# Sample states of an mLSTM step fetched two halves ahead, with GpSimd's stores and the memory input queued behind the last fetch

## The chip, the cores and the metric

The kernel runs on one core of one Trainium2 chip. The metric is device time in microseconds (us) of one execution; the time before is the median of three runs. Names of the engines in the profile: PE is TensorE (matmul; PEld its weight loads), DVE is VectorE, ACT is ScalarE, POOL is GpSimd, SP is SyncE, which here only issues DMAs.

## The reference

One layer of a hybrid decoder, in f32, on 256 prompt tokens and 8 sample tokens (one new token for each of 8 sequences), model width 2048. What matters here is the mLSTM of the sample tokens, four heads with keys of 128 and values of 256:

```python
def layer(x, conv_buf, h0, C0, n0, m0, mk, mv, ...):
    z = rmsnorm(x, g_mix) @ w_in                 # inputs of both head groups
    ... # causal conv, RG-LRU: y_rg
    q, k, v, logi, logf = ...                    # slices of z
    h_ml, C_new, n_new, m_new = mlstm(q, k, v, logi, logf, C0, n0, m0)
    y_ml = rmsnorm(h_ml, g_ml_out) * sigmoid(z[o])
    x = x + concat([y_rg, y_ml]) @ w_out
    x = x + cross_attention(rmsnorm(x, g_xa), mk, mv) @ w_xa_o
    x = x + (silu(xf @ w_ffn_gate) * (xf @ w_ffn_up)) @ w_ffn_down
# mlstm for one token, per sequence and head (sc, D from the gates):
#   C_new = sc * C + D * k v^T ;  n_new = sc * n + D * k
#   h = (q C_new) / max(|q n_new|, exp(-m))
```

The outputs are the prompt's and samples' activations and all new states, among them `o_sc` (C_new of the samples, 4 MB), `o_sn` (n_new), `o_h`, `o_cp`, `o_cs` (RG-LRU and conv states). The prompt's memory keys and values are made in the layer from `memT`; the samples' come from caches (`kcT`, `vcT`).

## The kernel before

The work is a list of steps on TensorE, one for each block of 128 output columns of a weight matrix (`w_in`, `w_out`, `w_q`, ...). A step reads 1 MB of weights, which SyncE loads as two halves of 512 KB (`raw`, five buffers). Each half is cast on ScalarE (`w<-raw`, the high part) and split on VectorE (`w<-raw,w`, the low part) into one of four `w` buffers; a product of f32 numbers is then three matmuls of high and low parts (`mm3`), 48 in a step. The splits of a step are made while the step before it runs.

All else is side work: generators (`rg_gen` for the RG-LRU, `ml_gates`, `ml_prompt`, `ml_values`, `ml_heads` and `ml_sample` for the mLSTM, `mem_gen` for the memory input, and others), from which `pump` takes pieces between steps by estimated times. A scheduler then orders the instructions of VectorE, ScalarE, GpSimd and TensorE by its own estimate; SyncE's stay as written. Each engine runs its instructions in the order so found, and a waiting one holds up all behind it. `tc.issue_after(x)` puts an instruction behind x. Tiles named `B` come from one pool of 26 buffers, so a DMA into a `B` waits until the buffer's last user is done.

`ml_prompt` makes, for each head, decay weights `E` (two `tensor_scalar`, one Exp, a mask product), the weighted scores `Pm` and the weighted keys `kw` (kept in `kb`); `ml_heads` multiplies `Pm` with the transposed values `vts`. Keys and values are kept in DRAM (`kept_k`, `kept_v`) for the prompt's state, which is made at the end of the kernel.

`ml_sample` works through the samples' states in eight halves, one for each head h and each group b4 of four sequences. It first writes the scaled keys `kd` and the queries of all heads and sequences as 64 rows to DRAM (`scr`). For a half, `fetch` then loads 512 KB of state (`C`, from `c0T`) and the half's key and query rows, each broadcast to all 128 partitions (`kq`, from `scr`). For each sequence ScalarE makes `dw` (two copies of the key row, scaled by a value), VectorE updates the state (`B<-B,bcs,dw`) and sums query times state twice (`ds<-B,B`); the new half goes out with `o_sc`. Before the change half n+1 is fetched when half n begins. All DMAs of this generator, and those of `memT`, `kcT`, `vcT`, are issued by GpSimd, whose queue is in order too.

Of the kernel before, what the change touches and what calls it, by code (L numbers as in the profile page):

```python
# [13 lines left out]
AF = mybir.ActivationFunctionType  # L14
# [3 lines left out]
P = 128  # L18
D = 2048
KC = D // P  # L20
T = 256
NS = 8
N = T + NS
RGB = 8
H = 4
# [17 lines left out]
STEP = object()  # L43
# [52 lines left out]
def layer_kernel(ctx: ExitStack, tc, xT, memT, vec, wrg, w_in, w_out, w_q, w_k, w_v, w_o,  # L96
# [3 lines left out]
    act, dve, pe = Engine(nc.scalar, price_act), Engine(nc.vector, price_dve), Engine(nc.tensor, price_pe)  # L100
    pool_e, sp = nc.gpsimd, nc.sync
# [17 lines left out]
    def B(shape, dt=F32):  # L119
        return sb.tile(shape, dt, tag="B", bufs=NB, name=nm("B"))  # L120
# [5 lines left out]
    def ltmp(w=N):  # L126
        return tmp(w, "lt")
# [381 lines left out]
    cpo = const.tile([P, RGB, 3], F32, name="cpo")  # L509
    cso = const.tile([P, RGB, NS, 3], F32, name="cso")  # L510
# [34 lines left out]
    def rg_gen():  # L545
# [41 lines left out]
        for q in range(2):  # L587
# [3 lines left out]
            act.activation(hlast[:, 4 * q: 4 * q + 4, :], h.tile(q)[:, :, T - 1: N], AF.Copy)  # L591
        pool_e.dma_start(o_h, hlast)
        pool_e.dma_start(o_cp, cpo)
        pool_e.dma_start(o_cs, cso)
        yield 0.3
# [190 lines left out]
    def ml_prompt():  # L786
# [13 lines left out]
        for h in range(H):  # L800
# [12 lines left out]
            dve.tensor_scalar(E[:, 256:384], bc[:, P:T], gcol[:, 1, h: h + 1], 0.0, op0=OP.add, op1=OP.min)  # L813
            act.activation(E, E, AF.Exp)
            if h == 0:
# [52 lines left out]
    def ml_sample():  # L868
# [3 lines left out]
        ks, qs = qk.tile(1)[:, :, T:N], qk.tile(0)[:, :, T:N]  # L872
        sc, Dg = bcs[:, :, 0:8], bcs[:, :, 8:16]
        x = ltmp(64)
        kd, qc = (x[:, o: o + 32].rearrange("p (h b) -> p h b", b=NS) for o in (0, 32))
        dve.tensor_mul(kd, ks, Dg)
        dve.tensor_copy(qc, qs)
        n0 = V("n0", 0, 32).rearrange("p (h b) -> p h b", b=NS)
        dve.tensor_mul(snew, n0, sc)
        dve.tensor_add(snew, snew, kd)  # L880
        pool_e.dma_start(o_sn, snew)

        dve.tensor_mul(ssum[:, 1], snew, qc)
        yield 0.6
# [9 lines left out]
        def fetch(h, b4):  # L894
            C, kq = B([P, 4, 2, P]), B([P, 2, 4, P])
            pool_e.dma_start(C, c0T[h, :, b4 * 4: b4 * 4 + 4])
            for j in range(2):
                r0 = j * 32 + h * 8 + b4 * 4
                src = scr[r0: r0 + 4, :].rearrange("b d -> (b d)")
                pool_e.dma_start(kq[:, j].rearrange("p b d -> p (b d)"), src.partition_broadcast(P))  # L900
            return C, kq

        ahead = fetch(0, 0)
        yield STEP
        for h in range(H):
            while ml.get("vn", 0) < 2 * h + 2 or "last" not in ml:
                yield STEP
            for b4 in range(2):
                C, kq = ahead
                n = 2 * h + b4 + 1  # L910
                if n < 2 * H:
                    ahead = fetch(n // 2, n % 2)
                for bb in range(4):
                    b = b4 * 4 + bb
                    t2 = sb.tile([P, 264], F32, tag="dw", bufs=2, name=nm("dw"))[:, 0: T]
                    t2 = t2.rearrange("p (v d) -> p v d", d=P)
                    for vb in range(2):
                        act.activation(t2[:, vb, :], kq[:, 0, bb, :], AF.Copy,
                                       scale=ml["v"](2 * h + vb)[:, T + b: T + b + 1])
                    with tc.issue_after(ml["last"].ins):  # L920
# [6 lines left out]
                    yield 0.8  # L927
                pool_e.dma_start(o_sc[h, :, b4 * 4: b4 * 4 + 4], C)
        yield 0.1
# [165 lines left out]
    def mem_gen():  # L1095
        raw = Arr(KC, T)
        for i in range(4):
            pool_e.dma_start(raw.tile(i), memT[:, i * 4: i * 4 + 4, :])
        yield STEP
# [375 lines left out]
    for i, (src, cols, pef, evf, need) in enumerate(steps):  # L1475
# [49 lines left out]
        if i == 57:  # L1525
            PACE["full"] = False
        if i == 44:
            pool_e.dma_start(kept_k, ml["kb"])
            for q in range(2):
                pool_e.dma_start(kept_v[q], ml["vts"][q])  # L1530
        if i == 40:
# [119 lines left out]
```

## Time and profile before

| | |
|---|---|
| median of three runs | 1449.22 us (1447.74 to 1449.48) |
| profiled execution | 1447.88 us, span of its trace 1445.9 us |
| TensorE busy | 1429.2 us (99%), clock granted 0.998 |
| VectorE, ScalarE, GpSimd busy | 1050.8 (73%), 796.9 (55%), 127.9 us (9%) |
| DMA | 329.17 MB, mean 228 GB/s |

Times inside the trace count from the start of the span. A row of the timeline gives the start, the time taken, engine, line, operation, out<-in by tile names, shape, how many alike follow each other, and in brackets how long the engine had idled before and what ended that. Most rows have line 61, that of a helper which records every operation, so tiles tell more than lines.

### The profile page before, as it was taken

How to read it: one execution, taken by the hardware profiler on the slowest of the kernel's cores; microseconds unless marked ns; L12 is line 12 of the kernel's file. 1: busy time of each engine (PE TensorE's matmuls, PEld its weight loads, DVE VectorE, ACT ScalarE, POOL GpSimd, SP SyncE). 2: the span in 40 equal slices, each digit the busy share in tenths (PEclk: the TensorE clock that was granted, in tenths of full speed). 3: DMA queues.
4: the chain of work that ended last, by engine and by line, in shares of the span. 5: the costliest groups of instructions: out<-in, count | busy, mean ns of one | idle time of the engine just before them, and what ended most of it. 6: DMA issues, size and time to landing. Idle time of an engine off the chain costs nothing.

```text
span 1445.9 us, 29975 instructions
## 1 busy us (share of the span) xinstructions
PE 1429.2 (99%) x11979; PEld 1405.4 (97%) x11979; DVE 1050.8 (73%) x2014; ACT 796.9 (55%) x1289; POOL 127.9 (9%) x203
## 2 busy tenths in 40 slices
PE   9999999999999999999999999999999999999997
PEld 9999899999999999899999999999999999999997
DVE  7967798998899999977676656555665655556565
ACT  7678786765556666655544444434444434444474
POOL 0001220000225433300000000000000000000000
PEclk9999999999999999999999999999999999999999
DMA  9745897557789887856555555555555555555573
GB/s 291 235 172 188 297 361 277 176 177 274 280 334 383 318 303 263 338 173 216 193 194 197 194 198 195 194 200 192 196 198 190 201 193 192 201 191 197 169 239 128
DMA packets 100764, 329.17 MB, mean 228 GB/s; under 512 B 11056, under 2 KB 19936, under 8 KB 100624
## 3 DMA queue, kind: packets, MB, share of 16 engines
q1 hardware_dynamic: 84480, 272.09, 54.2%
q0 software_dynamic: 15424, 54.22, 10.1%
q8 instruction: 93, 1.52, 0.4%
q10 hardware_dynamic: 720, 0.95, 0.2%
q14 instruction: 47, 0.39, 0.1%
HBM read 314.36 MB, written 12.86 MB: 226 GB/s over the span
## 4 chain that ended last, share of the span: by engine, by line
PE 56%; DVE 1%; issue 1%; DMA 0%; ACT 0%; POOL 0%; DVEq 0%; POOLq 0%; ACTq 0%
PE mm L61 56%; PE ax L61 1%; DVE B L61 1%; DVE dw L61 0%; DMA o_v<-B 0%; POOL ds L1200 0%; DVE w L61 0%; DVE t L61 0%; ACT B L61 0%; ACT dw L61 0%; ACT t L61 0%; DVE ax L61 0%; ACT ds L61 0%; DVE rstd L61 0%; DVEq L1628 0%
## 5 line engine op out<-in xcount | busy, mean ns | idle before, releaser
L61 PE MATMUL mm<-B,w 128*128 128x264 f32 (+1 forms) x10960 | 1281.9, 279 | 1.8 <-DVE w L61 1.7
L61 PEld LDWEIGHTS mm<-B,w 128*128 128x128 f32 x10960 | 1261.3, 189 | 9.9 <-DVE w L61 2.3
L61 DVE TENSOR_TENSOR w<-raw,w 128x1024 fp32r<-128x1024 f32 (+1 forms) x522 | 625.2, 1200 | 299.0 <-ACT w L61 298.3
L61 ACT ACTIVATE w<-raw 128x1024 fp32r<-128x1024 f32 (+1 forms) x522 | 534.8, 1028 | 514.6 <-PE mm L61 353.3
L61 PE MATMUL mm<-w,B 128*128 128x512 f32 x384 | 86.9, 380 | 0.1
L61 PEld LDWEIGHTS mm<-w,B 128*128 128x128 f32 x384 | 70.7, 190 | 9.6 <-DVE w L61 0.5
L1542 POOL TENSOR_TENSOR B<-B,rstd 128x264 f32<-128x264 f32 x4 | 2.8, 735 | 802.0 <-ACT B L61 802.0
L61 DVE TENSOR_TENSOR t<-mm,rstd 128x264 f32<-128x264 f32 x96 | 41.6, 434 | 28.4 <-PE mm L61 28.3
L61 DVE SCALAR_TENSOR_TENSOR B<-B,dw 128x256 f32<-128x256 f32 x128 | 54.3, 478 | 3.2 <-ACT dw L61 3.0
L61 DVE TENSOR_TENSOR xres<-xres,mm 128x264 f32<-128x264 f32 (+1 forms) x81 | 34.2, 424 | 24.6 <-PE mm L61 24.6
L61 DVE SCALAR_TENSOR_TENSOR dw<-B,qsm,dw 128x256 f32<-128x256 f32 x96 | 48.7, 513 | 2.4 <-ACT dw L61 1.6
L61 PE MATMUL ax<-B,B 128*128 128x256 f32 (+3 forms) x276 | 44.6, 302 | 1.9 <-DVE B L61 1.0
L1200 POOL TENSOR_TENSOR ds<-dw,ds 128x256 fp32r<-128x256 f32 x32 | 35.6, 1114 | 107.1 <-ACT ds L61 107.0
L61 PEld LDWEIGHTS ax<-B,B 128*128 128x128 f32 x276 | 38.0, 191 | 4.7 <-DVE B L61 1.6
L61 ACT ACTIVATE B<-xres,vecs 128x264 fp32r<-128x264 f32 (+1 forms) x64 | 32.2, 503 | 4.5 <-DVE xres L61 2.7
L61 ACT ACTIVATE dw<-B,qsm 128x256 f32<-128x256 f32 x32 | 16.3, 508 | 24.6 <-issue 10.5
L1189 POOL DMA_DIRECT2D B<-kcT x32 | 17.3, 542 | 139.1 <-DVE B L61 126.2
L61 ACT ACTIVATE t<-xres 128x264 f32<-128x264 f32 (+1 forms) x53 | 21.0, 408 | 14.0 <-DVE xres L61 13.9
L61 ACT ACTIVATE dw<-B,B 128x128 f32<-128x128 f32 x64 | 21.2, 393 | 11.8 <-DMA B<-scr 8.5
L61 DVE SCALAR_TENSOR_TENSOR B<-xres,vecs,B 128x264 fp32r<-128x264 f32 x48 | 23.4, 489 | 4.1 <-ACT B L61 4.1
L61 ACT ACTIVATE dw<-ax,dw 128x256 f32<-128x256 f32 x32 | 15.0, 469 | 18.8 <-DVE dw L61 17.8
L61 ACT ACTIVATE B<-t 128x264 fp32r<-128x264 f32 (+1 forms) x60 | 24.1, 409 | 1.8 <-DVE t L61 1.8
(182 smaller groups left out, 684.9 us busy)
## 6 DMA issues: line engine op xcount, KB each, us to landing
raw<-w_gu SPq DMA_DIRECT2D x176, 512.0 KB, 4.1
raw<-w_d SPq DMA_DIRECT2D x80, 512.0 KB, 3.9
raw<-w_in SPq DMA_DIRECT2D x74, 512.0 KB, 5.2
raw<-w_out SPq DMA_DIRECT2D x32, 512.0 KB, 4.0
raw<-w_q SPq DMA_DIRECT2D x32, 512.0 KB, 5.9
B<-kcT POOLq DMA_DIRECT2D x32, 512.0 KB, 8.7
B<-vcT POOLq DMA_DIRECT2D x32, 512.0 KB, 10.0
raw<-w_k SPq DMA_DIRECT2D x32, 512.0 KB, 5.1
```

Source lines behind the costliest of these rows:

```text
L61: return f(*a, **k)
L1189: pool_e.dma_start(kc, kcT[h, b])
L1200: pool_e.tensor_sub(ws[:, 1], acc, ws[:, 0].bitcast(F32))
L1542: e.tensor_mul(st["y"](c), st["y"](c), r)
```

## The change

The states of the first two halves are loaded at the start of `ml_sample`, as soon as the gates are there. The key and query rows are laid out so that one broadcast DMA brings both for a half. Two fetches run ahead; the next one is issued behind a half's work, and the half's store `o_sc` behind that fetch. The first use of the rows on ScalarE (`dw`) stands behind the first Exp of `ml_prompt`. The stores of kept keys and values, of `o_h`, `o_cp`, `o_cs` and `o_sn` move behind the last `o_sc`, and the loads of memory input behind the last kept store.

```diff
@@ rg_gen
-        pool_e.dma_start(o_h, hlast)
-        pool_e.dma_start(o_cp, cpo)
-        pool_e.dma_start(o_cs, cso)
@@ ml_prompt
-            act.activation(E, E, AF.Exp)
+            ml.setdefault("exp", act.activation(E, E, AF.Exp))
@@ ml_sample
+        def load(h, b4):
+            C = B([P, 4, 2, P])
+            pool_e.dma_start(C, c0T[h, :, b4 * 4: b4 * 4 + 4])
+            return C
+
+        loaded = [load(0, 0), load(0, 1)]
         x = ltmp(64)
-        kd, qc = (x[:, o: o + 32].rearrange("p (h b) -> p h b", b=NS) for o in (0, 32))
+        kd = ltmp(32).rearrange("p (h b) -> p h b", b=NS)
...
         dve.tensor_mul(kd, ks, Dg)
-        dve.tensor_copy(qc, qs)
+        dve.tensor_copy(x4[:, :, :, 0], by4(kd))
+        dve.tensor_copy(x4[:, :, :, 1], by4(qs))
...
-        pool_e.dma_start(o_sn, snew)
...
         def fetch(h, b4):
-            C, kq = B([P, 4, 2, P]), B([P, 2, 4, P])
-            pool_e.dma_start(C, c0T[h, :, b4 * 4: b4 * 4 + 4])
-            for j in range(2):
-                r0 = j * 32 + h * 8 + b4 * 4
-                src = scr[r0: r0 + 4, :].rearrange("b d -> (b d)")
-                pool_e.dma_start(kq[:, j].rearrange("p b d -> p (b d)"), src.partition_broadcast(P))
+            C = loaded.pop(0) if loaded else load(h, b4)
+            kq = B([P, 2, 4, P])
+            r0 = (2 * h + b4) * NS
+            src = scr[r0: r0 + NS, :].rearrange("b d -> (b d)")
+            ml["fetch"] = pool_e.dma_start(kq.rearrange("p j b d -> p (j b d)"), src.partition_broadcast(P))
             return C, kq
 
-        ahead = fetch(0, 0)
+        ahead = [fetch(0, 0), fetch(0, 1)]
...
-                C, kq = ahead
-                n = 2 * h + b4 + 1
-                if n < 2 * H:
-                    ahead = fetch(n // 2, n % 2)
+                C, kq = ahead.pop(0)
+                n = 2 * h + b4 + 2
                 for bb in range(4):
...
-                    for vb in range(2):
-                        act.activation(t2[:, vb, :], kq[:, 0, bb, :], AF.Copy,
-                                       scale=ml["v"](2 * h + vb)[:, T + b: T + b + 1])
+                    with tc.issue_after(ml["exp"].ins):
+                        for vb in range(2):
+                            act.activation(t2[:, vb, :], kq[:, 0, bb, :], AF.Copy,
+                                           scale=ml["v"](2 * h + vb)[:, T + b: T + b + 1])
...
-                pool_e.dma_start(o_sc[h, :, b4 * 4: b4 * 4 + 4], C)
+                if n < 2 * H:
+                    ahead.append(fetch(n // 2, n % 2))
+                with tc.issue_after(ml["fetch"].ins):
+                    last = pool_e.dma_start(o_sc[h, :, b4 * 4: b4 * 4 + 4], C)
+        while min(ml.get("pn", 0), ml.get("vtn", 0)) < H:
+            yield STEP
+        with tc.issue_after(last.ins):
+            pool_e.dma_start(kept_k, ml["kb"])
+            for q in range(2):
+                ml["kept"] = pool_e.dma_start(kept_v[q], ml["vts"][q])
+            pool_e.dma_start(o_h, hlast)
+            pool_e.dma_start(o_cp, cpo)
+            pool_e.dma_start(o_cs, cso)
+            pool_e.dma_start(o_sn, snew)
@@ mem_gen
-            pool_e.dma_start(raw.tile(i), memT[:, i * 4: i * 4 + 4, :])
+            with tc.issue_after(ml["kept"].ins):
+                pool_e.dma_start(raw.tile(i), memT[:, i * 4: i * 4 + 4, :])
@@ layer_kernel, the loop over the steps
-        if i == 44:
-            pool_e.dma_start(kept_k, ml["kb"])
-            for q in range(2):
-                pool_e.dma_start(kept_v[q], ml["vts"][q])
```

What this does to the order on the engines. GpSimd's queue before, from the rows' store to the third half's fetch (`c0T` loads a state, the loads from `scr` bring its rows, one DMA for keys and one for queries):

```order
L892 DMA scr_1803<-lt_197_1801 64x128
L896 DMA B_208_1881<-c0T 128x1024
L900 DMA B_209_1882<-scr_1803 128x512 x2
L592 DMA o_h<-hlast_94 128x72
L896 DMA B_219_1977<-c0T 128x1024
L900 DMA B_220_1978<-scr_1803 128x512 x2
L1530 DMA kept_v_106<-B_177_1625 128x1032
L928 DMA o_sc<-B_208_1881 128x1024
L1528 DMA kept_k_105<-B_187_1708 128x1024
L928 DMA o_sc<-B_219_1977 128x1024
L896 DMA B_266_2272<-c0T 128x1024
L900 DMA B_267_2273<-scr_1803 128x512 x2
```

The same place after, and on to the store of the third half (`B_267`) with the sixth half's row (`B_328`) behind it:

```order
L874 DMA B_179_1629<-c0T 128x1024
L874 DMA B_180_1631<-c0T 128x1024
L897 DMA scr_1808<-lt_200_1806 64x128
L904 DMA B_211_1886<-scr_1808 128x1024
L904 DMA B_212_1888<-scr_1808 128x1024
L874 DMA B_267_2267<-c0T 128x1024
L904 DMA B_268_2269<-scr_1808 128x1024
L934 DMA o_sc<-B_179_1629 128x1024
...
L874 DMA B_327_2641<-c0T 128x1024
L934 DMA o_sc<-B_267_2267 128x1024
L904 DMA B_328_2643<-scr_1808 128x1024
```

The third half's fetch now stands ahead of the first state store and of both kept stores; a later row, the sixth half's, stands behind the third half's store. On ScalarE before, around the first Exp of `ml_prompt` (the row `B_207<-B_207`), with the first half's `dw` copies ahead of two weight casts:

```order
L61 ACTIVATE B_177_1625<-ax_196_1795 128x2x256
L61 ACTIVATE dw_221_1982<-B_209_1882,B_180_1636 128x128 x2
L61 ACTIVATE dw_237_2077<-B_209_1882,B_180_1636 128x128 x2
L61 ACTIVATE w_210_1887<-raw_193_1773 128x8x128
L61 ACTIVATE hlast_94<-B_204_1872 128x36
L61 ACTIVATE w_211_1890<-raw_194_1775 128x8x128
L61 ACT_TABLE_LOAD
L61 ACTIVATE B_207_1880<-B_207_1880 128x384
L61 ACTIVATE B_187_1708<-B_186_1707,B_207_1880 128x128 x2
```

And after:

```order
L61 ACTIVATE B_177_1625<-ax_199_1800 128x2x256
L61 ACTIVATE w_213_1891<-raw_196_1778 128x8x128
L61 ACTIVATE hlast_94<-B_207_1877 128x36
L61 ACTIVATE w_214_1894<-raw_197_1780 128x8x128
L61 ACT_TABLE_LOAD
L61 ACTIVATE B_210_1885<-B_210_1885 128x384
L61 ACTIVATE dw_222_1978<-B_211_1886,B_183_1641 128x128 x2
L61 ACTIVATE dw_238_2073<-B_211_1886,B_183_1641 128x128 x2
L61 ACTIVATE B_190_1713<-B_189_1712,B_210_1885 128x128 x2
```

The four `dw` copies moved from ahead of the two weight casts to behind the Exp. On VectorE the order changes only from the fourth half on; where the seventh half is updated (`B_350` before, `B_351` after), before the change, from one weight split to the next:

```order
L61 TENSOR_TENSOR w_345_2755<-raw_324_2644,w_345_2755 128x8x128
L61 SCALAR_TENSOR_TENSOR ds_364_2904,nums_108<-B_326_2649,B_327_2650 128x128
L61 SCALAR_TENSOR_TENSOR B_350_2815<-B_350_2815,bcs_96,dw_378_2993 128x256
L61 SCALAR_TENSOR_TENSOR ds_366_2911,nums_108<-B_326_2649,B_327_2650 128x128
L61 TENSOR_TENSOR acc_rg_95<-acc_rg_95,t_333_2672 128x264
L61 TENSOR_TENSOR t_343_2748<-mm_336_2681,rstd_91 128x264
L61 SCALAR_TENSOR_TENSOR B_350_2815<-B_350_2815,bcs_96,dw_387_3066 128x256
L61 SCALAR_TENSOR_TENSOR ds_364_2904,nums_108<-B_326_2649,B_327_2650 128x128
L61 TENSOR_TENSOR w_346_2758<-raw_325_2646,w_346_2758 128x8x128
```

After, the last twelve rows ahead of the split that corresponds to the one after those:

```order
L61 SCALAR_TENSOR_TENSOR ds_365_2895,nums_108<-B_327_2641,B_328_2643 128x128
L61 SCALAR_TENSOR_TENSOR ds_367_2902,nums_108<-B_327_2641,B_328_2643 128x128
L61 TENSOR_TENSOR B_207_1877<-B_207_1877,t_344_2740 128x264
L61 SCALAR_TENSOR_TENSOR ds_378_2980,nums_108<-B_351_2806,B_352_2808 128x128
L61 SCALAR_TENSOR_TENSOR B_351_2806<-B_351_2806,bcs_96,dw_388_3056 128x256
L61 SCALAR_TENSOR_TENSOR ds_380_2987,nums_108<-B_351_2806,B_352_2808 128x128
L61 SCALAR_TENSOR_TENSOR B_351_2806<-B_351_2806,bcs_96,dw_390_3063 128x256
L61 SCALAR_TENSOR_TENSOR ds_378_2980,nums_108<-B_351_2806,B_352_2808 128x128
L61 TENSOR_TENSOR acc_rg_95<-acc_rg_95,t_345_2744 128x264
L61 SCALAR_TENSOR_TENSOR ds_380_2987,nums_108<-B_351_2806,B_352_2808 128x128
L61 SCALAR_TENSOR_TENSOR ds_389_3060,nums_108<-B_351_2806,B_352_2808 128x128
L61 TENSOR_TENSOR w_347_2750<-raw_326_2639,w_347_2750 128x8x128
```

Eleven of the seventeen operations that stand between two splits there are shown; before, seven stand between the two.

More of the change, by code (lines that the diff above doesn't have):

```diff
@@ L873, in ml_sample @@
         sc, Dg = bcs[:, :, 0:8], bcs[:, :, 8:16]
+        def load(h, b4):
[3 more added lines that the diff above has]
+        loaded = [load(0, 0), load(0, 1)]
         x = ltmp(64)
-        kd, qc = (x[:, o: o + 32].rearrange("p (h b) -> p h b", b=NS) for o in (0, 32))
+        kd = ltmp(32).rearrange("p (h b) -> p h b", b=NS)
+        by4 = lambda t: t.rearrange("p h (g b) -> p h g b", b=4)
+        x4 = x.rearrange("p (h g j b) -> p h g j b", g=2, j=2, b=4)
         dve.tensor_mul(kd, ks, Dg)
-        dve.tensor_copy(qc, qs)
+        dve.tensor_copy(x4[:, :, :, 0], by4(kd))
+        dve.tensor_copy(x4[:, :, :, 1], by4(qs))
         n0 = V("n0", 0, 32).rearrange("p (h b) -> p h b", b=NS)
@@ L880, in ml_sample @@
         dve.tensor_add(snew, snew, kd)
-        pool_e.dma_start(o_sn, snew)
-        dve.tensor_mul(ssum[:, 1], snew, qc)
+        dve.tensor_mul(ssum[:, 1], snew, qs)
         yield 0.6
```

## The prediction

> **What bounds the kernel now.** I read the page's busy times first, then the busy time by stage, then what TensorE waits for, then the rows of the engines that it waits for.
>
> ```profile
> PE 1429.2 (99%) x11979; PEld 1405.4 (97%) x11979; DVE 1050.8 (73%) x2014; ACT 796.9 (55%) x1289; POOL 127.9 (9%) x203
> ```
>
> TensorE is busy for 1429.2 of 1445.9 us, so a change elsewhere can only win what is in its gaps. By stage (columns: stretch, length, PE, PEld, DVE, ACT, POOL busy, clock, DMA share, GB/s):
>
> ```profile
> 100.00:140.00 40.00, 39.55 (x335) 38.80 (x335) 25.28 (x47) 33.15 (x62) 4.87 (x9) 1.00 0.49 165
> 140.00:180.00 40.00, 38.05 (x302) 36.25 (x301) 30.00 (x86) 28.60 (x72) 8.51 (x16) 1.00 0.87 295
> 180.00:220.00 40.00, 38.24 (x331) 37.44 (x330) 40.00 (x143) 32.70 (x78) 9.10 (x17) 1.00 0.97 366
> 220.00:260.00 40.00, 40.00 (x359) 40.00 (x358) 33.07 (x76) 23.66 (x36) 0.00 (x0) 1.00 0.69 248
> ```
>
> The sample states are worked through in the second and third rows. TensorE idles 0.45 + 1.95 + 1.76 = 4.16 us in 100 to 220, and not at all after it. The list of its waits from 100 to 240 us has 4.1 us, and its own rows show where they lie:
>
> ```profile
> PE mm L61 <- DVE w L61: 1.7, 2, 1.5
> PE ax L61 <- DVE B L61: 1.5, 3, 0.7
> PE ax L61 <- ACT B L61: 0.9, 1, 0.9
> ```
> ```profile
> 139.74 0.66 PE L61 MATMUL ax<-ident,B 128*128 128x128 f32 x4 [0.45 <-DVE B L61]
> 148.02 1.14 PE L61 MATMUL ax<-B,B 128*128 128x258 f32 x4 [0.39 <-DVE B L61]
> 158.86 1.14 PE L61 MATMUL ax<-B,B 128*128 128x258 f32 x4 [0.65 <-DVE B L61]
> ...
> 170.61 5.65 PE L61 MATMUL mm<-B,w 128*128 128x264 f32 x48
> 177.11 1.57 PE L61 MATMUL ax<-B,B 128*128 128x258 f32 x6 [0.86 <-ACT B L61]
> ...
> 195.50 11.68 PE L61 MATMUL mm<-B,w 128*128 128x264 f32 x96 [0.15 <-DVE w L61]
> 208.71 16.24 PE L61 MATMUL mm<-B,w 128*128 128x264 f32 x142 [1.53 <-DVE w L61]
> ```
>
> Six gaps, 0.45 + 0.39 + 0.65 + 0.86 + 0.15 + 1.53 = 4.03 us: the most that this change can remove. Behind them stand two waits of ScalarE for a broadcast row (`B<-scr`, the `kq` tile):
>
> ```profile
> 135.21 1.28 ACT L61 ACTIVATE dw<-B,B 128x128 f32<-128x128 f32 x4 [3.56 <-DMA B<-scr]
> 136.39 1.04 ACT L61 ACTIVATE w<-raw 128x1024 fp32r<-128x1024 f32 x1
> ...
> 173.77 1.28 ACT L61 ACTIVATE dw<-B,B 128x128 f32<-128x128 f32 x4 [4.96 <-DMA B<-scr]
> 174.96 1.04 ACT L61 ACTIVATE w<-raw 128x1024 fp32r<-128x1024 f32 x1
> ...
> 176.49 0.57 ACT L61 ACTIVATE B<-ax 128x512 f32<-128x512 f32 x1
> ```
>
> Behind each wait stands the cast of a weight half, which VectorE then splits; after the second also the copy (176.49) that TensorE waits for at 177.11. VectorE takes the delay over:
>
> ```profile
> 137.47 1.23 DVE L61 TENSOR_TENSOR w<-raw,w 128x1024 fp32r<-128x1024 f32 x1 [1.55 <-ACT w L61]
> ...
> 174.50 1.07 DVE L61 SCALAR_TENSOR_TENSOR B<-B,bcs,dw 128x256 f32<-128x256 f32 x2 [4.43 <-ACT dw L61]
> ...
> 207.41 1.25 DVE L61 TENSOR_TENSOR w<-raw,w 128x1024 fp32r<-128x1024 f32 x1
> 208.55 0.51 DVE L61 SCALAR_TENSOR_TENSOR B<-B,bcs,dw 128x256 f32<-128x256 f32 x1
> 208.94 0.31 DVE L61 SCALAR_TENSOR_TENSOR ds<-B,B 128x128 f32<-128x128 f32 x1
> 209.15 0.11 DVE L61 DVE_READ_ACCUMULATOR ds<-B,B 128x1 f32 x1
> ```
>
> After 4.43 idle us at 174.5 it is busy without a break through 180 to 220 (40.00 above), and the split that starts at 207.41 is the one that TensorE waits for at 208.71.
>
> **Why the second row was late.** GpSimd's queue, where the DMA issues wait in order:
>
> ```profile
> 156.30 0.54 POOL L928 DMA_DIRECT2D o_sc<-B  x1 [8.58 <-DVE B L61]
> 161.42 0.53 POOL L1528 DMA_DIRECT2D kept_k<-B  x1 [4.58 <-ACT B L61]
> 163.66 0.53 POOL L928 DMA_DIRECT2D o_sc<-B  x1 [1.71 <-DVE ds L61]
> 164.19 0.53 POOL L896 DMA_DIRECT2D B<-c0T  x1
> 164.71 1.08 POOL L900 DMA_DIRECT2D B<-scr  x2
> ```
>
> The third half's two fetches stand behind two state stores and a `kept_k` store, each waiting for its data; they issue at 164.19 and 164.71, only 4 us before ScalarE wants the row (173.77 − 4.96 = 168.81).
>
> **The change part by part.** *First use behind the Exp.* The four `dw` copies of the first half move behind ScalarE's first Exp. The 3.56 us wait goes, and the cast at 136.39 can run as soon as its `w` buffer and weights are there. VectorE then starts the split of 137.47 up to 1.55 us earlier. From that split on VectorE and ScalarE hand work to each other, so the lead should last to the gaps at 139.74, 148.02 and 158.86. These need 0.45, 0.84 and 1.49 us of lead in turn, since TensorE itself comes earlier by what the gaps before gave. Late next: the `dw` copies, 1.28 us of ScalarE, now stand between the Exp and the two key copies. They delay the key copies only, which nothing waits for before the store at the end. The bounds: none of the 1.49 (another wait takes over) or all of it. I take 0.45 + 0.39 + half of 0.65 = 1.16, as a lead of 1.55 against a need of 1.49 leaves nothing for a slip.
>
> *The third fetch no longer behind `kept_k` and the stores.* In the new order the third half's two fetches stand ahead of the first state store. What they wait for then is a free buffer: by the program's buffers, the end of the last head's score matmuls, here the group at 154.83.
>
> ```profile
> 154.83 0.82 PE L61 MATMUL ax<-B,B 128*128 128x256 f32 x4
> ...
> DMA to landing us min/median/max: 3.9/10.6/14.6
> ```
>
> So they issue at about 156. The second line is the time to landing of the row fetches (and of the rows' own store) before. In the new order nothing else is queued ahead of them by then, so the low end is nearest, with 512 KB in one DMA in place of two of 256 KB; even the median gives 167, before 168.81. The 4.96 us wait goes, and with it the 0.86 us gap. VectorE starts the third half 4.43 us earlier. How much of that is left where TensorE waited? The new order on VectorE puts four updates, nine sums and four other operations between two weight splits, where it had fewer. By the spacing of the rows above (1.14 split, 0.39 update, 0.21 sum) and 0.35 taken for the others, between the two, this is 1.14 + 1.56 + 1.89 + 1.40 = 6.0 us, and adding up all operations since 174.50 in the two orders the split after it stands 2.4 us later than before, the next one 0.4 us later. TensorE uses up a split in 5.65 / 2 = 2.83 us. The split of 207.41 was 1.53 us late; with 4.43 − 0.4 = 4.0 us of lead, less 1.0 us by which TensorE comes earlier (0.86 + 0.15), it is 1.5 us early. The one before it gets 4.43 − 2.4 − 1.0 = 1.0 us more than it had, and it was in time. So I take all of 0.86 + 0.15 + 1.53 = 2.54; the bounds are 0 and 2.54.
>
> *States fetched earlier, one broadcast in place of two.* Two state fetches go out ahead of the rows' store and no longer behind it; the DMA share in 100 to 140 was 0.49, so the weight loads hide them, at nothing. Were that cover gone, a load would come a few us later, with the casts ahead of TensorE by a whole step. Eight issues of 0.54 us go from GpSimd, which was 9% busy. One small copy more on VectorE (below 0.3 us) falls in a stage where it is 25.28 of 40 us busy: nothing.
>
> *Stores moved behind the last state store.* `kept_k`, both `kept_v`, `o_h`, `o_cp`, `o_cs`, `o_sn`, then memory input: about 1.7 MB of stores come ahead of the four memory loads. What was there:
>
> ```profile
> 218.92 0.53 POOL L1098 DMA_DIRECT2D B<-memT  x1 [5.74 <-ACT t L61]
> 267.63 0.40 ACT L61 ACTIVATE lt<-B 128x256 f32<-128x256 f32 x1
> 220.00:230.00 10.00, 10.00 (x92) 10.00 (x91) 6.82 (x15) 6.57 (x8) 0.00 (x0) 1.00 1.00 390
> 230.00:240.00 10.00, 10.00 (x92) 10.00 (x91) 9.86 (x25) 7.45 (x15) 0.00 (x0) 1.00 0.58 193
> ```
>
> The memory input is first read at 267.63, nearly 50 us after the last issue. At 390 − 193 = 197 GB/s beside the weights the extra 1.7 MB take some 9 us, so the memory input comes by about 236. Its cover is those 30 us; nothing else waits for these stores. The weight loads share the transfers in this stretch without a gap on TensorE at 390 GB/s, so I price them at nothing.
>
> The sum: 1.16 + 2.54 = 3.7 us. Against the profiled execution (1447.88 us, span 1445.9) that is 1444.2; this execution lies 1.34 us below the median of the three runs, 1449.22, so the median to expect is 1445.5 us, 0.26% less.
>
> **The rivals.** *Only the later gaps go* (chance 0.22). If the head's chain of Exp, scores and PSUM banks sets the three early gaps, the lead of 1.55 us is lost and 2.54 us remain: 1446.7. For it speaks that the last two of them come 12 and 23 us after ScalarE's wait; against it that all three end on VectorE, which is 30.00 of 40 us busy there.
>
> *VectorE takes it back* (0.11): after 340 us it is the fuller engine.
>
> ```profile
> 400.00:460.00 60.00, 60.00 (x469) 58.06 (x468) 58.09 (x149) 36.10 (x61) 22.21 (x33) 1.00 0.95 354
> 460.00:520.00 60.00, 60.00 (x331) 54.15 (x330) 58.49 (x147) 37.87 (x75) 23.62 (x28) 1.00 0.82 304
> 520.00:600.00 80.00, 79.58 (x481) 72.62 (x480) 76.68 (x197) 51.23 (x102) 29.21 (x45) 1.00 0.88 333
> ```
>
> If it were bound there by something that doesn't start earlier, all 3.7 us would turn into a wait of TensorE near 590 to 620: 1449.2. Against it: that work starts with the queries, which TensorE paces, and 220 to 260 leaves VectorE 7 us to fall into step.
>
> *A fetch behind a store* (0.10). The sixth half's row now stands behind the third half's store, and the eighth's behind the fourth's. With the third half started at 174.50 − 4.43 = 170.1, its updates end near 176, where the sixth row is issued; adding up the operations in the new order, ScalarE needs it near 187, eleven microseconds later. If it lands later, ScalarE waits with weight casts behind it, as at 173.77, and all of the wait beyond the 1.0 to 1.5 us of lead comes back as gaps. At the longest landing, 14.6, that is 3.6 − 1.2 = 2.4 us of the 3.7 gained: 1447.9. From about 19 us on it decides: 8 us of wait are 6.7 us of gaps, 3.0 more than the gain, 1452.2. For it speaks the DMA share of 0.97 in 180 to 220; against it that fetches of two halves leave this stretch.
>
> *More is hidden than the gaps show* (0.02). The PEld column falls short by 1.20 + 3.75 + 2.56 = 7.5 us in 100 to 220, against 4.16 in the PE column; if all of it were lost time that the change gives back, the time would be 1441.7. Against it: 48 matmuls take 5.65 us in the disturbed stretch at 170.61, and the products in plain f32 that stand between them run long on one weight load, so I trust the gaps. [...] No run here shows yet which of the two the time follows.
>
> *It doesn't do what it says* (0.05): the buffer for the third half is not free before 164, and the fetch stays where it was. Then only the early 1.16 remain: 1448.1.
>
> **How the numbers follow.** The forecast, both terms, has 0.50; its own range is 1444.3 (all 4.03 us, and a little of the runs' spread) to 1446.6. A difference under 0.2%, 2.9 us, is about what a measurement of this kernel can't tell from none. The forecast lies on the fast side of that bound in five of six cases, the first rival in three of ten: faster 0.42 + 0.07, and 0.02 for the hidden time, roughly 0.50. Slower: the third rival with a landing past 19 us, 0.06. Same: the rest, 0.44. The range 1443.9 to 1449.3 takes in the first two rivals, the third at the longest landing seen and the fourth; it leaves out the slower end and the 7.5 us of the weight loads.
>
> **What would show it.** Right: no wait of ScalarE for `B<-scr`; VectorE's idle time before the third half gone; the third fetch issued before 157; no gap of TensorE over 0.3 us from 130 to 215; the same stage rows after 400. Wrong: a wait for `B<-scr` near 185 or 200, a gap near 590 to 620, a wait for `raw` in 210 to 240, or the early three gaps still there.

## The result: 0.5% faster, twice what was forecast

The changed kernel takes 1441.53 us (median of five runs, 1441.14 to 1442.52), the kernel before 1449.16 in the same series: ratio 0.995, 95% interval 0.9939 to 0.9961. That is 7.6 us less, where 3.7 were forecast (1445.5, range 1443.9 to 1449.3). The profiled execution after took 1442.52 us (span 1439.5), the one before 1447.88 (span 1445.9).

The busy times of the profile after, then the stages 100 to 220 us by the same columns as before, then all waits of TensorE:

```profile
PE 1426.8 (99%) x11979; PEld 1404.9 (98%) x11979; DVE 1050.3 (73%) x2015; ACT 796.5 (55%) x1289; POOL 124.1 (9%) x195
```
```profile
100.00:140.00 40.00, 40.00 (x342) 39.43 (x341) 26.83 (x51) 33.10 (x61) 1.67 (x3) 1.00 0.49 167
140.00:180.00 40.00, 39.35 (x320) 38.19 (x320) 34.34 (x105) 34.18 (x93) 7.38 (x14) 1.00 0.82 282
180.00:220.00 40.00, 40.00 (x356) 39.81 (x354) 37.38 (x124) 29.70 (x61) 9.03 (x17) 1.00 0.97 368
```
```profile
PE ax L61 <- ACT w L61: 1.4, 2, 1.1
PE mm L61 <- DVE pad L61: 1.1, 1, 1.1
PE ax L61 <- DVE B L61: 0.7, 1, 0.7
PE ax L61 <- ACT t L61: 0.3, 1, 0.3
```

Of the six gaps between 130 and 220 one is left, the 0.65 us of the head products, now at 157.49. VectorE is no longer full from 180 to 220 (37.38 of 40). The third half's fetch issues behind the last score matmuls, ahead of the first state store, and ScalarE starts the half without a wait:

```profile
154.57 0.53 POOL L874 DMA_DIRECT2D B<-c0T  x1 [21.51 <-PE ax L61]
155.09 0.53 POOL L904 DMA_DIRECT2D B<-scr  x1
155.61 0.54 POOL L934 DMA_DIRECT2D o_sc<-B  x1
```
```profile
167.35 1.26 ACT L61 ACTIVATE dw<-B,B 128x128 f32<-128x128 f32 x4
...
187.18 1.26 ACT L61 ACTIVATE dw<-B,B 128x128 f32<-128x128 f32 x4
...
198.52 1.26 ACT L61 ACTIVATE dw<-B,B 128x128 f32<-128x128 f32 x4
```

To see where the time went I matched each weight split of VectorE with the same split in the other trace and took the difference of their starts. The changed kernel is 0.25 us later at 111 us, 5.23 earlier at 277, and 6.68 earlier from 650 to the end. So 5.48 us come from the stage 111 to 277 and 1.45 from 277 to 650, where nothing was expected. The rest up to 7.6 lies in the spread of executions: the start of the kernel, up to 111 us, differs by up to 1.7 us between traces whose order there is nearly the same.

The gain in the late stage has a cause that stands in the rows of before. GpSimd there, before:

```profile
571.77 0.56 POOL L1189 DMA_DIRECT2D B<-kcT  x1
574.47 0.53 POOL L1193 DMA_DIRECT2D B<-vcT  x1 [2.13 <-issue]
574.99 0.53 POOL L1189 DMA_DIRECT2D B<-kcT  x1
```

and after (that trace is 5.6 us earlier there):

```profile
566.16 0.55 POOL L1206 DMA_DIRECT2D B<-kcT  x1
566.70 0.54 POOL L1210 DMA_DIRECT2D B<-vcT  x1
567.23 0.53 POOL L1206 DMA_DIRECT2D B<-kcT  x1
...
581.38 0.57 POOL L1268 DMA_DIRECT2D o_k<-t  x1
584.43 0.54 POOL L1206 DMA_DIRECT2D B<-kcT  x1 [2.49 <-issue]
```

Some 2 us in which GpSimd waits for nothing that the profile shows stand ahead of the 54th load of `kcT` or `vcT` before, and ahead of the 61st after. Counted along its queue both are the 115th DMA issue; the change has eight issues fewer ahead of it. (Another unexplained stretch, 4.05 us at 404.04 before and 4.04 at 398.81 after, stays with its load.) Behind the 2 us before the change, key loads landed late (the 57th load at 588.89 us, against 585.46 in the changed kernel; table below), and TensorE waited for the samples' scores:

```profile
585.22 0.38 PE L61 MATMUL ax<-ds,onesr 128*128 128x256 f32 x1 [0.24 <-ACT ds L61]
...
588.63 0.38 PE L61 MATMUL ax<-ds,onesr 128*128 128x256 f32 x1 [0.17 <-POOL ds L1200]
```
```profile
619.29 0.38 PE L61 MATMUL ax<-ds,onesr 128*128 128x256 f32 x1 [0.24 <-POOL ds L1200]
```

None of these three waits is left after the change.

### The profile page after: what moved, and what is told of

It is laid out like the page before. It is cut to its first block, busy times and chain, and to the rows that moved or that the text cites. A ratio compares the mean times of both kernels' runs of the same rounds, so it can differ in the third digit from the quotient of the medians.

```text
span 1439.5 us, 29961 instructions
## 1 busy us (share of the span) xinstructions
PE 1426.8 (99%) x11979; PEld 1404.9 (98%) x11979; DVE 1050.3 (73%) x2015; ACT 796.5 (55%) x1289; POOL 124.1 (9%) x195
## 3 DMA queue, kind: packets, MB, share of 16 engines
q8 instruction: 93, 1.52, 0.4%
## 4 chain that ended last, share of the span: by engine, by line
PE 69%; DVE 1%; issue 0%; ACT 0%; POOL 0%; DVEq 0%; POOLq 0%; ACTq 0%
PE mm L61 67%; PE ax L61 2%; DVE B L61 0%; DVE w L61 0%; DVE dw L61 0%; POOL ds L1217 0%; DVE t L61 0%; ACT w L61 0%; ACT t L61 0%; DVE ax L61 0%; ACT dw L61 0%; ACT ds L61 0%; DVE rstd L61 0%; DVE osm L61 0%; DVEq L1641 0%
## 5 line engine op out<-in xcount | busy, mean ns | idle before, releaser
L61 ACT ACTIVATE ds<-dw 128x256 fp32r<-128x256 f32 x32 | 13.3, 415 | 21.8 <-DVE dw L61 21.8
```

Of the source, the lines that this page charges most:

```text
L61: return f(*a, **k)
```

## The experiments

Shifts are against the trace of before, in us (minus is earlier), over the two stages; the last two columns are what TensorE's two columns lack of 130 us from 110 to 240. "115th issue" tells which of the loads of `kcT` and `vcT` is the 115th DMA on GpSimd's queue. All traces are single ones: a wait of 0.4 us near 436 that comes and goes between kernels of the same order (below) moves the second stage by that much.

| kernel | median (before beside it) | ratio, 95% | 111 to 277 | 277 to 650 | 115th issue | PE idle | PEld idle |
|---|---|---|---|---|---|---|---|
| before | | | 0 | 0 | 54th | 4.15 | 7.25 |
| changed | 1441.53 (1449.16) | 0.9939 to 0.9961 | -5.48 | -1.45 | 61st | 0.65 | 2.31 |
| first use only | 1446.46 (1448.94) | 0.9975 to 0.9992 | -2.09 | +0.73 | 54th | 2.54 | 5.21 |
| two ahead only | 1451.08 (1448.94) | 1.0008 to 1.0026 | +1.18 | +0.40 | 54th | 5.14 | 8.53 |
| stores only | 1446.94 (1448.85) | 0.9977 to 0.9994 | -0.41 | -0.87 | 54th | 3.66 | 6.86 |
| one row only | 1448.98 (1448.94) | 0.9990 to 1.0008 | +1.52 | -1.43 | 61st | 5.39 | 8.78 |
| changed, no first use | 1444.03 (1448.94) | 0.9954 to 0.9979 | -3.42 | -1.41 | 61st | 1.96 | 4.30 |
| changed, stores back | 1448.70 (1448.85) | 0.9993 to 1.0010 | +3.19 | -1.81 | 61st | 5.31 | 7.79 |
| changed, two rows | 1442.21 (1448.07) | 0.9945 to 0.9972 | -5.83 | -1.31 | 54th | 0.65 | 2.11 |
| changed, 8 DMAs more | 1443.70 (1448.85) | 0.9952 to 0.9977 | -5.49 | -0.74 | 54th | 0.65 | 2.31 |
| changed, 14 memsets more | 1441.37 (1448.85) | 0.9934 to 0.9962 | -5.49 | -1.81 | 61st | 0.65 | 2.30 |

**First use alone, and all but the first use.**

```diff
 before
-            act.activation(E, E, AF.Exp)
+            ml.setdefault("exp", act.activation(E, E, AF.Exp))
...
+                    with tc.issue_after(ml["exp"].ins):
                         for vb in range(2):
                             act.activation(t2[:, vb, :], kq[:, 0, bb, :], AF.Copy, ...)
```

> The kernel before with only the first use of the rows behind the first Exp; nothing else moves on any engine. Theory A (a removed wait is worth its gap in the TensorE column): the gaps at 139.74 and 148.02 go, 0.45 + 0.39 = 0.84 us, that at 158.86 stays. Theory B (a wait costs the time from one matmul's start to the next beyond the usual spacing, about 0.16 us more than its gap, and delays too short to be called gaps count too): 1.63 us, the shift that the changed kernel shows between 131 and 150. Both leave the rows after 170 and those of 560 to 620 as before: the 115th DMA issue of GpSimd's queue still is a vcT load near 573 with some 2 us of idle time ahead of it.

The other kernel takes that `issue_after` out of the changed one.

> The changed kernel without its first step: the dw copies of the first half stand ahead of the two weight casts again, all else as changed. Theory A: 0.84 us slower than the changed kernel, 1442.4. Theory B: 1.63 us slower, 1443.2. Rival F: the rows land 3 us later (136.3) than the casts need, so that ScalarE's wait is as long as before and its delay runs on into the third half: 2 to 4 us slower than changed. The stage from 560 to 620 stays as in the changed kernel.

The step is worth 2.09 us put into the kernel before and 5.48 - 3.42 = 2.06 taken out of the changed one; by the medians 2.5 both times. The gaps speak of 0.84. Without it the three waits are there again, and the first two gaps (0.85 and 0.38) make up 1.23 of the 2.06:

```profile
140.53 0.66 PE L61 MATMUL ax<-ident,B 128*128 128x128 f32 x4 [0.85 <-DVE B L61]
148.82 1.14 PE L61 MATMUL ax<-B,B 128*128 128x258 f32 x4 [0.38 <-DVE B L61]
159.66 1.14 PE L61 MATMUL ax<-B,B 128*128 128x258 f32 x4 [0.66 <-DVE B L61]
```

In the kernel before, a gap went with it that both theories had left alone, the 0.86 us at 177.11: the third fetch issued at 163.08 in place of 164.19, and ScalarE waited 0.74 us less for its row.

```profile
171.93 1.28 ACT L61 ACTIVATE dw<-B,B 128x128 f32<-128x128 f32 x4 [4.22 <-DMA B<-scr]
175.27 1.57 PE L61 MATMUL ax<-B,B 128*128 128x258 f32 x6
```

So the gaps that went there are 0.45 + 0.39 + 0.86 = 1.70 of the 2.09. By 150 us 1.60 of the 2.09 were gained, where A had 0.84 and B 1.63: A falls, and B is right up to there; the rest came after 170, where both had nothing. Taken out of the changed kernel the step is worth 0.4 us more than B's 1.63. F's 2 to 4 us hold, its mechanism does not: all of the 2.06 is lost by 150 us, and the delay does not run on into the third half. What the first use brings and what the rest brings add up, 2.09 + 3.42 = 5.51 against 5.48.

**Two halves ahead alone.** The first two states loaded with the gates, `fetch` two ahead behind a half's work and the store behind it; two broadcasts, stores where they were.

```diff
 before
-        ahead = fetch(0, 0)
+        ahead = [fetch(0, 0), fetch(0, 1)]
...
+                if n < 2 * H:
+                    ahead.append(fetch(n // 2, n % 2))
+                with tc.issue_after(ml["fetch"].ins):
                     pool_e.dma_start(o_sc[h, :, b4 * 4: b4 * 4 + 4], C)
```

> The kernel before with only the fetch of two halves ahead (first two states with the gates, a next fetch behind a half's work, the store behind it); rows still as two broadcasts, stores of kept keys and values and of the states where they were, first use not moved. Theory A (gaps): 0.86 + 0.15 + 1.53 = 2.54 us. Theory B (start to start): 3.85 us, what the changed kernel gains between 159 and 225. Rival C: with the kept stores still between the fetches, the third fetch waits behind them, and less than 1.3 us is gained. The 115th issue of GpSimd's queue is as before, so nothing more is gained in 560 to 620.

It is slower, 1451.08. Rival C held, and more: the third fetch stands behind the store of kept keys, which waits 13.71 us for ScalarE's key copies.

```profile
162.07 0.54 POOL L1536 DMA_DIRECT2D kept_k<-B  x1 [13.71 <-ACT B L61]
162.60 0.54 POOL L877 DMA_DIRECT2D B<-c0T  x1
163.12 1.08 POOL L907 DMA_DIRECT2D B<-scr  x2
```

**Stores alone.** The kernel before with the moves of `kept_k`, `kept_v`, `o_h`, `o_cp`, `o_cs`, `o_sn` behind the last `o_sc`, and of the memory loads behind these.

```diff
 before
-        if i == 44:
-            pool_e.dma_start(kept_k, ml["kb"])
...
+        with tc.issue_after(last.ins):
+            pool_e.dma_start(kept_k, ml["kb"])
...
```

> The kernel before with only the stores moved behind the last o_sc and the memory input behind them. The third fetch still stands behind the second o_sc, which waits for VectorE until 163.7. Theory G (order of fetch and stores both needed): the fetch issues near 164 as before, within 0.7 us of before, 1448.9. Rival I (the kept stores alone held it up): the third fetch issues at 159 to 161 and 2.5 us are gained, 1446.4. The 115th issue is at the 54th of the kcT and vcT loads as before: no gain in 560 to 620.

The third fetch issues at 165.32, near the 164 that G said: it waits behind the second state store.

```profile
164.80 0.54 POOL L923 DMA_DIRECT2D o_sc<-B  x1 [6.81 <-DVE ds L61]
165.32 0.53 POOL L891 DMA_DIRECT2D B<-c0T  x1
```

Its 1.9 us by the medians (1.3 by the traces), where G allowed 0.7, are not the fetch's, which is no earlier than before; VectorE's order moved in 16 rows, the 1.53 us gap near 208 is gone and one of 0.57 has come near 231. The early fetch and the moved stores are worth +1.18 and -0.41 us alone and, with one row in place of two, -3.42 together.

**Changed, with only the stores put back** (the reverse of the diff above).

> The changed kernel with only its moved stores put back: kept keys and values, o_h, o_cp, o_cs and o_sn where they were, and the memory input not held. Theory G (the stores had to move for the early fetch to be worth anything): the third fetch stands behind the store of kept keys, issues near 160 and not 154.6, and what was gained between 159 and 225 in the changed kernel is lost again: 2.5 to 3.9 us slower than changed, 1444 to 1445.4. Rival H (fetching two ahead alone does it): within 0.7 us of the changed kernel, 1441.5. The 115th issue stays the kcT load that is the 61st of the kcT and vcT loads, so the stage of 560 to 620 stays as in the changed kernel.

All is lost, 1448.70 us. The fetch issues at 160.66 as G said; but the size is twice G's. The prediction's rival of a fetch behind a store is what happens here: with the second `kept_v` and the stores in between, the rows land up to 21 us after their issue, and ScalarE waits 2.60, 1.51 and 1.71 us at the third, fourth and fifth half and 3.88 us at the seventh. Behind this last wait TensorE waits twice:

```profile
160.13 0.53 POOL L1538 DMA_DIRECT2D kept_k<-B  x1 [13.70 <-ACT B L61]
160.66 0.53 POOL L877 DMA_DIRECT2D B<-c0T  x1
```
```profile
199.44 0.69 ACT L61 ACTIVATE dw<-B,B 128x128 f32<-128x128 f32 x2 [3.88 <-DMA B<-scr]
```
```profile
202.03 0.49 PE L61 MATMUL mm<-B,w 128*128 128x264 f32 x2 [2.57 <-ACT w L61]
203.77 5.65 PE L61 MATMUL mm<-B,w 128*128 128x264 f32 x24 [1.25 <-DVE w L61]
```

The second row is long for 24 matmuls (48 took 5.65 us before, at 170.61). The windows say why; the third figure from the end is the granted clock:

```profile
202.00:204.00 2.00, 0.73 (x3) 0.53 (x4) 2.00 (x7) 1.46 (x5) 0.00 (x0) 0.78 0.78 315
204.00:206.00 2.00, 2.00 (x10) 2.00 (x11) 2.00 (x12) 1.70 (x5) 0.53 (x1) 0.50 0.73 238
206.00:208.00 2.00, 2.00 (x11) 2.00 (x11) 2.00 (x13) 1.88 (x5) 0.00 (x0) 0.50 0.84 342
208.00:210.00 2.00, 2.00 (x11) 1.89 (x11) 2.00 (x9) 2.00 (x5) 0.00 (x0) 0.52 0.03 12
```

In a stretch of 2.57 + 1.25 us of idle time with two matmuls between, the granted clock fell to half (0.50) and stayed there until 210: it withheld (0.22 + 0.50 + 0.50 + 0.48) x 2 = 3.4 us. In the first row TensorE was busy for 0.73 us only, so some 0.3 of these lie in the gap of 1.25 us, and about 3.1 us were lost beside the gaps, a good part of what this kernel loses beyond G's 3.9. What makes the clock fall is not shown.

**One row alone.**

```diff
 before
...
-            for j in range(2):
-                r0 = j * 32 + h * 8 + b4 * 4
-                src = scr[r0: r0 + 4, :].rearrange("b d -> (b d)")
-                pool_e.dma_start(kq[:, j].rearrange("p b d -> p (b d)"), src.partition_broadcast(P))
+            r0 = (2 * h + b4) * NS
+            src = scr[r0: r0 + NS, :].rearrange("b d -> (b d)")
+            pool_e.dma_start(kq.rearrange("p j b d -> p (j b d)"), src.partition_broadcast(P))
```

The part left out lays the rows of `scr` out as in the changed kernel.

> The kernel before with only the rows as one broadcast in place of two: eight issues fewer on GpSimd, the order of the rest nearly the same. By the prediction nothing is gained (within 0.5 us). Theory D (the 2 us of idle time ahead of the 115th issue on GpSimd goes by the count of issues, not by the place in the program): it moves from the vcT load near 574 to the kcT load near 589, the loads between come some 2 to 3 us earlier, the waits of TensorE for ds at 585, 588, 616 and 619 go, and 1.0 to 1.45 us are gained in 560 to 620. Rival E: that idle time goes by the state of the engines; then it stays near 574 and nothing is gained there.

The median says nothing gained, as predicted, and hides two things that cancel: 1.52 us lost by 277, where TensorE waits 1.99 us at 178.16 (0.86 at 177.11 before), and 1.43 gained after it. The idle time of GpSimd moved to the 61st load, as D said, so E falls:

```profile
591.75 0.54 POOL L1191 DMA_DIRECT2D B<-kcT  x1 [2.46 <-issue]
```

**Eight DMAs more; 14 memsets more; two rows again.** Each is the changed kernel; in the first two the order of every engine but GpSimd is that of the changed kernel.

```diff
 changed, mem_gen, behind the loads of memory input in the code
+        with tc.issue_after(ml["kept"].ins):
+            for q in range(8):
+                pool_e.dma_start(drm.tile([P, 4], F32, name=f"pad{q}"), ones[:, 4 * q: 4 * q + 4])
```
```diff
 changed, same place
+        with tc.issue_after(ml["kept"].ins):
+            fill = const.tile([P, 16], F32, name="fill")
+            for q in range(14):
+                pool_e.memset(fill[:, q: q + 1], 0.0)
```

> The changed kernel with eight small stores (2 KB each, of a constant) on GpSimd's queue ahead of the loads of memory input; the order on every other engine is the same. Theory D (idle time ahead of the 115th issue, by count): it stands ahead of the 54th kcT or vcT load again, near 569, the loads behind it come 2 us later, TensorE waits for ds again and the time is 1.1 to 1.45 us more than changed, about 1442.8. Rival J (by the instructions in GpSimd's stream, not its DMAs): with eight to sixteen instructions more it moves there too; this run alone doesn't tell D from J. Rival K (the gain in 560 to 620 came from another shift of the engines): no change, 1441.5.

> The changed kernel with 14 memsets of one column on GpSimd at the same place, and no DMA more: its instruction stream is as long as before the change, its count of DMA issues as in the changed kernel. Theory D (count of DMA issues): the idle time stays ahead of the 61st kcT or vcT load near 584, 1441.5. Rival J (place in the instruction stream): it stands ahead of the 54th load, and the time is 1.1 to 1.45 us more, 1442.8.

> The changed kernel with the rows as two broadcasts for each half again: eight issues more on GpSimd, all else as changed. Theory D: the idle time ahead of the 115th issue is at the 54th kcT or vcT load again; of the stage from 277 to 650 us, where the changed kernel gains 1.45 us, 0.7 to 1.45 are lost. Between 111 and 277 us the prediction's price for one broadcast was nothing: there it gains 5.5 us over before as the changed kernel does, and the whole is 0.7 to 1.5 us slower than changed, 1442.2 to 1443. Rival M (the second broadcast ahead of each half also holds up the rows): 1 to 3 us of the 5.5 are lost as well, 1443.2 to 1446.

The idle time's place, with eight DMAs more, with 14 memsets more, with two rows:

```profile
568.87 0.54 POOL L1213 DMA_DIRECT2D B<-vcT  x1 [2.15 <-issue]
```
```profile
584.90 0.54 POOL L1210 DMA_DIRECT2D B<-kcT  x1 [2.48 <-issue]
```
```profile
569.90 0.54 POOL L1211 DMA_DIRECT2D B<-vcT  x1 [2.14 <-issue]
```

Of its place D is right: in all eleven kernels of the table it stands ahead of the 115th DMA issue (2.13 to 2.49 us in the six whose rows are given here), and 14 instructions that are no DMAs don't move it, so J falls. Nor does it go by the packets: GpSimd's DMA queue had moved 13,253 of them by 574 us before, and 14,064 by 584 us after. Of its price D was too sure: two rows have the idle time at the 54th load as well and lose nothing by it (their median, 0.7 us above the changed kernel's, is within D's range, but the trace doesn't show it in this stage). The loss goes with the time at which the loads behind it land. On TensorE's own time (each trace shifted so that the group at 578.25 of before coincides), with the landing of the 57th load, the start of the last of the samples' score matmuls that waited, and how much later than 617.58 that is:

```text
kernel                   115th   57th load lands   score matmul   lost
changed                  61st    585.46            617.58         0
one row only             61st    585.58            617.58         0
changed, memsets         61st    585.38            617.58         0
changed, no first use    61st    586.38            617.58         0
changed, stores back     61st    586.06            617.58         0
changed, two rows        54th    586.44            617.63         0.05
stores only              54th    587.86            618.43         0.85
changed, 8 DMAs          54th    588.18            618.55         0.97
two ahead only           54th    588.85            619.27         1.69
before                   54th    588.89            619.29         1.71
first use only           54th    589.71            619.64         2.06
```

With the idle time at the 61st load nothing is lost in five kernels of five; at the 54th the loads land up to 4 us later, and past about 586.4 each later landing costs more, up to 2 us. So the change won 1.71 us here. Its eight issues fewer are enough for that, as one row alone shows, but they are not needed: with two rows the changed kernel loses 0.05. What made the loads land earlier there is not shown, and so K, a shift of another kind, falls for the eight DMAs (0.97 lost) but not for the change as a whole. In this trace 0.36 of the gain was lost again at 436.58, where TensorE waits 0.4 us for a `ds` in the weight-load column; with the 14 memsets, in the same order, that wait is not there. By the medians the eight DMAs cost more, 2.2 us against the changed kernel and 2.3 against the memsets, than the 1.0 of the traces; what the rest is stays open. M falls: the second broadcast costs nothing in the first stage (-5.83 us with two rows, -5.48 with one).

**What a wait costs, by itself.** Late in the kernel, where TensorE has no gap, 20 waits were put in, and in a twin the same instructions without the dependence (`ident` for `z`). Neither changes what is computed.

```diff
 changed, the loop over the steps
...
+        if 20 < n_end <= 100 and n_end % 4 == 0:
+            z, g2 = ltmp(P), bank("ax")
+            act.activation(z, ps[:, 0:P], AF.Copy)
+            pe.transpose(g2[:, 0:P], z, ident)
         ps = pef(i)
```

The part left out is the same in both: TensorE keeps the written order over the last 102 steps.

> The changed kernel with 20 waits put into the last 100 steps, where TensorE runs without a gap: ahead of every fourth step ScalarE copies 128 columns of the step's product before it (z), TensorE transposes the copy into a bank that nobody reads, and only then starts the step. To be compared with the same kernel without the dependence. Each wait should show a gap of 0.3 to 0.8 us in TensorE's rows, G in all. Theory A (a wait costs its gap): the twin is faster by G. Theory B (a gap counts from the modelled end of the last matmul, 276 ns after its start, where the next would have started after 112 ns): faster by G + 20 x 0.164 = G + 3.3 us, and each wait reads as a start-to-start distance of gap + 276 ns.

> The twin: the same 20 copies on ScalarE and the same 20 transposes on TensorE, but of the constant identity, so that TensorE waits for nothing. Against the changed kernel it costs the 20 transposes, 20 x 0.11 to 0.22 us (the rows of 128-column transposes), 2.2 to 4.4 us: 1443.7 to 1445.9; no gap of TensorE after 900.

With waits 1475.08 us, without 1443.88: 31.2 us. The list of waits, and the stages that hold the 20 steps, with waits and without:

```profile
PE ax L61 <- ACT lt L61: 27.1, 20, 1.6
```
```profile
900.00:1360.00 460.00, 432.90 (x3811) 429.03 (x3810) 246.45 (x285) 185.48 (x227) 0.00 (x0) 1.00 0.51 181
```
```profile
895.00:1360.00 465.00, 465.00 (x4136) 465.00 (x4135) 268.42 (x312) 201.75 (x247) 0.00 (x0) 1.00 0.56 193
```

The gaps add up to 27.1 us. B's sum is 30.4, and the weight-load column lacks 460 - 429.03 = 31.0. The matched splits are 31.5 us apart, (31.5 - 27.1) / 20 = 0.22 us for each wait beyond its gap: 0.164 is B's difference between the 276 ns of a matmul's row and the 112 ns from one start to the next (247 in a row take 27.95 us at 879.77 with the waits), and the rest is in the first matmul behind a wait, 0.33 us long here against 0.27 in the twin:

```profile
909.03 0.33 PE L61 MATMUL ax<-ident,lt 128*128 128x128 f32 x1 [1.31 <-ACT lt L61]
```
```profile
907.89 0.27 PE L61 MATMUL ax<-ident 128*128 128x128 f32 x1
```

A is refuted by 4 us. These waits of 1.3 to 1.6 us, 23 us apart, left the clock at 1.00.

**The last gap.** In the changed kernel the generator of the head products waits one step more (`yield STEP` once more ahead of each head's products).

> The changed kernel with the generator of the head products (ml_heads) taken up one step later, to take away the one gap left between 100 and 600 us, 0.65 us at 157.49. Theory B: 0.8 us faster than the changed kernel, 1440.7, with no gap there. Theory A: 0.65 us. Rival L: the new order moves VectorE's and ScalarE's work as well (some 100 rows), and puts as much waiting elsewhere between 150 and 260: no gain, 1441.5 or more. The 115th issue stays where it is.

1442.51 us (0.9946 to 0.9971 of before), a microsecond more than the changed kernel had: L. The gap at 157 is gone; the head products wait 0.29 us at 154.12 in its place, and gaps for a split have come at 203.65 (0.18 us) and 303.55 (0.44 us). No version here beats the changed kernel beyond what the runs can tell.

## Why the prediction was wrong

*The step that failed first: "4.03 us: the most that this change can remove".* It took the gap column for the time lost. The same stage gave 5.48 us with one of the gaps, 0.65, still there. Five gaps of 3.38 us went; at 0.22 us more for each they are 4.5, and the remaining 1.0 lies, as far as can be read, in start-to-start distances too short to show as gaps, such as 0.33 us near 147 and 148 and 0.43 at 195.5 where 0.11 is usual. The rival that I gave 0.02, more hidden than the gaps show, was nearest: its column fell short by 7.5 us and by 2.6 after, 4.9 less. That its time, 1441.7, is the measured one within 0.2 us is luck in part: 2.6 us of the shortfall stayed, and 1.45 us came from a stage of which it says nothing. In the table the change of the PEld shortfall gives the shift of the first stage within 0.1 us for the first use (-2.04 against -2.09), two ahead (+1.28, +1.18), stores (-0.39, -0.41) and one row (+1.53, +1.52), and within 0.7 for the others whose clock held; the PE column is off by up to 2.3 us. So the time followed the weight-load column here, and my reason against it, the plain f32 products, was beside the point: these are there before and after.

*First use behind the Exp, 1.16 us.* Right in mechanism: the waits at 139.74 and 148.02 went; the one at 158.86 stayed whole, where I took half of it. Mis-sized: 2.1 us. Put into the kernel before it also took the gap at 177.11, which my sum gave to the third fetch alone.

*The third fetch, 2.54 us.* Right in place (predicted about 156, it was 154.57) and in what follows; mis-sized: 3.4 us. It needs both the fetch and the stores moved; either alone brings next to nothing by this road.

*A fetch behind a store.* The sixth half's row was predicted to issue near 176 and to be needed near 187: 176.51 and 187.18 in the trace. It landed at 186.6, and the eighth half's at 198.34 against a need at 198.52. So this rival missed by 0.6 and 0.2 us, which is near to luck: the eighth row took 17.0 us to land, and the longest that I had gone by was 14.6. The kernel with the stores put back shows it happening, with a price that I had not named, the halved clock (0.50; about 3.1 us beside the gaps).

*Priced at nothing.* One broadcast for two: right for the first stage; but the eight issues that it saves moved GpSimd's idle time, which alone gave 1.43 us in the late stage (one row only). The memory input came 4 us later than before (last landing 230.3) and nothing waited.

*"The same stage rows after 400."* Wrong by 1.45 us: 1.71 gained where GpSimd's idle time stood, 0.36 lost at 436, and 0.1 of reading. That row of before, 574.47 with 2.13 us that nothing explains, was there to be read; that it goes by the count of issues could not be.

## What to carry to other kernels

Where TensorE is the bound, price a stall by what its weight-load column lacks, or by start-to-start distances, not by the gaps alone: each of the 20 waits put in cost its gap and 0.22 us (27.1 us of gaps, 31.0 lacking in the weight-load column, 31.2 lost), and others seem to have cost time without showing a gap. Before fetching further ahead, look at what stands ahead of the fetch in its in-order queue; the early fetch gained only with the stores out of its way (alone it lost 1.18 us, behind a store that waited 13.71). And when a count of DMA issues changes, look for idle time that moves with it far from the edit (here some 2 us, which cost up to 2.06 us where it stood at the 54th load).

## What the runs showed of the hardware

GpSimd idled ahead of its 115th DMA issue in all eleven kernels of the table, whether that loads `kcT` or `vcT`: for 2.13 to 2.49 us, between 568.87 and 591.75 us, in the six whose rows are given here. 14 instructions of another kind did not move it (61st load, 2.48 us), and eight small DMAs did (54th load, 2.15 us). Why is not shown. TensorE's granted clock fell to 0.50 for nearly 7 us in and after a stretch of 2.57 and 1.25 us of idle time with two matmuls between (stores back); waits of 1.3 to 1.6 us 23 us apart (20 waits), and a single one of 1.99 (one row alone), left it at 1.00.
